# A two-layer hybrid encoder: tiles moved by 64 bytes, S5 tables made by doubling, norm rows stored from ScalarE's queue, first raw weights in freed slots

## The chip, the cores and the metric

The kernel runs on one core of one Trainium2 chip. Its engines are TensorE (PE in the profile; PEld is its weight load), VectorE (DVE), ScalarE (ACT), GpSimd (POOL) and SyncE (SP), which issues most DMAs. The metric is the device time of one execution in microseconds, as the median of several runs.

## The reference, cut to what matters

Two layers, 512 rows of 1024. Four mixers read x, a gate weights each, a projection and a layer norm follow, then a SwiGLU FFN of width 2816 and a second layer norm.

```python
h = x @ w_in[l]
branches = (o_ret, o_att, o_gla, o_s5)
mixed = sum(sigmoid(x @ w_gate[l, b] + b_gate[l, b]) * (branches[b] @ w_branch[l, b]) for b in range(4))
x = layer_norm(ALPHA * x + mixed @ w_out[l], ln1_g[l], ln1_b[l])
ffn = (silu(x @ w_ffn_gate[l]) * (x @ w_ffn_up[l])) @ w_ffn_down[l]
x = layer_norm(ALPHA * x + ffn, ln2_g[l], ln2_b[l])
# in o_s5, a diagonal complex state: ab = mag * exp(i * theta), x[t] = ab * x[t-1] + bu[t]
```

For S5 the kernel uses tables of cos and sin of t * theta for t = 0 to 511, in 8 groups of 128 states (`er`, `ei`).

## The kernel before, in words

Every float32 product is made of three products of a high part and a rest in the format fp32r (`wh` and `wl` for a weight, `XH` and `XL` for x): `split` (L202) writes the high part on ScalarE (a CAST) and the rest on VectorE. Weights come by `wload` (L343): a DMA into `wr` (two buffers) on SyncE's queue, then the split into `wh` and `wl`, which a priority puts ahead of other work; the Tile scheduler orders the rest by dependence and by the order of the code. Each engine, and SyncE's queue, works in that fixed order.

A layer goes through these stages. *Mixers and gates* (`phase("mx", MIXERS)`, L1178): projections, four mixers and a stream of gate products `pg` and branch products `pb`, which add up in 8 tiles `acc`. *Projection* `proj_ln` (L508) with `wo`: 8 slices k, four blocks t of 128 rows, products `pj`; the last 4 slices are done block by block, with `layer_norm` (L417) after each block. Its `rest` (L449) stores the normalised rows to `xsp` in DRAM, transposes them on TensorE (`tp`), scales them (`xf`) and splits them into `XH` and `XL`; `block_sums` (L479) makes from the blocks the operands `bh`, `bl` of a Strassen-like scheme. *FFN* `ffn` (L1069): 22 slices f; `weights` (L1077) loads `raw` (128x2048) and `ws` (128x1024, to which a second, adding DMA on GpSimd's queue comes), makes `s24` on GpSimd and splits into `wh`/`wl` (twice), `wkh`/`wkl` and `fh`/`fl`; `product` (L1104) is 12 matmuls of 256 columns, of which each slice has seven (`fa`, `fb`, `fc`). The heads of the first two slices (`PRE = 2`) stand ahead of the rest; that of the first needs only `raw` and the first two blocks of x. *Down-projection*: `proj_ln` with `wdn`, 22 slices k, the operands `aph`, `apl` split from the FFN's `g`. In layer 0 it also makes layer 1's S5 tables, by `tables(k)` (L1167): `s5_constants(1)` at k = 0, then at each even k from 2 to 16 `s5_table` on GpSimd, out of a table of 32 and one of 16 angles (`eb`, `ea`) that `s5_constants` (L244) leaves to GpSimd. The two results are stored to `esp` in DRAM from SyncE's queue (L1173).

Tiles lie in pools; a phase's pool begins behind the pools that are always there. Before the change, `XH`, `XL`, the pairs `b` and all tiles of the phases (`fh`, `fl`, `wkh`, `wkl`, `aph`, `apl`, the `a` slots) begin at a multiple of 128 bytes in each partition, `wr`, `wh` and `wl` 64 bytes past one.

## Time and profile before

| | |
|---|---|
| median of 3 runs | 1786.33 us (1785.63 to 1788.24) |
| the profiled execution | 1790.67 us, its span 1788.8 us |
| PE, PEld, DVE, ACT, POOL busy | 92%, 84%, 68%, 40%, 31% of the span |
| mean granted TensorE clock | 0.962 of full speed |

The profile is of one execution; its span goes from the first to the last instruction. Engines overlap, so their shares don't add up. A row of the timeline gives the start, the duration, the instruction (output<-inputs, x count for several in a row), and in brackets the idle time before it and what ended it. Most rows name L126, the helper that records operations, so rows are told apart by tiles. All times of all views are in us from the span's start.

### The profile page before, as it was taken

How to read it: one execution, taken by the hardware profiler on the slowest of the kernel's cores; microseconds unless marked ns; L12 is line 12 of the kernel's file. 1: busy time of each engine (PE TensorE's matmuls, PEld its weight loads, DVE VectorE, ACT ScalarE, POOL GpSimd, SP SyncE). 2: the span in 40 equal slices, each digit the busy share in tenths (PEclk: the TensorE clock that was granted, in tenths of full speed). 3: DMA queues.
4: the chain of work that ended last, by engine and by line, in shares of the span. 5: the costliest groups of instructions: out<-in, count | busy, mean ns of one | idle time of the engine just before them, and what ended most of it. 6: DMA issues, size and time to landing. Idle time of an engine off the chain costs nothing. (4 is left out here: it accounts for less than half of the span.)

```text
span 1788.8 us, 27714 instructions
## 1 busy us (share of the span) xinstructions
PE 1641.2 (92%) x11068; PEld 1503.4 (84%) x11068; DVE 1224.6 (68%) x1801; ACT 711.1 (40%) x1200; POOL 550.4 (31%) x503
## 2 busy tenths in 40 slices
PE   8999998989969999984799999999999689999997
PEld 7988887878859999963589989888898589999786
DVE  4766468988587777671364656689876777786635
ACT  4453342233354444420243554533333444444321
POOL 0601015650043444189400000022204534442602
PEclk9999999989989999996899999999999899999999
DMA  6522212222357767322435423134333577773522
GB/s 204 186 93 82 79 60 73 85 90 95 112 172 203 226 202 223 100 101 94 141 120 193 155 70 121 58 95 136 114 106 132 168 207 206 217 209 116 177 95 82
DMA packets 82785, 241.46 MB, mean 135 GB/s; under 512 B 8352, under 2 KB 8544, under 8 KB 77024
## 3 DMA queue, kind: packets, MB, share of 16 engines
q1 hardware_dynamic: 70688, 216.63, 35.7%
q0 software_dynamic: 11968, 23.07, 7.5%
q8 instruction: 86, 1.41, 0.3%
q14 instruction: 43, 0.35, 0.1%
HBM read 220.79 MB, written 18.87 MB: 134 GB/s over the span
## 5 line engine op out<-in xcount | busy, mean ns | idle before, releaser
L126 DVE TENSOR_TENSOR wl<-wr,wh 128x1024 fp32r<-128x1024 f32 (+2 forms) x162 | 205.0, 1267 | 296.9 <-ACT wh L126 284.8
L126 ACT CAST wh<-wr 128x1024 fp32r<-128x1024 f32 (+2 forms) x162 | 164.9, 1020 | 360.8 <-PE pg L126 103.8
L126 PE MATMUL pg<-XH,wh 128*128 128x256 f32 x1024 | 150.1, 288 | 1.3 <-DVE sg L126 1.2
L126 PE MATMUL pg<-XL,wh 128*128 128x256 f32 x1024 | 146.9, 284 | 0.0
L126 PEld LDWEIGHTS pg<-XH,wh 128*128 128x128 f32 x1024 | 139.7, 196 | 8.5 <-DVE sg L126 2.6
L126 PE MATMUL pg<-XH,wl 128*128 128x256 f32 x1024 | 144.9, 282 | 0.0
L126 PE MATMUL pj<-wh,aph 128*128 128x512 f32 x320 | 106.8, 409 | 39.4 <-ACT wh L126 37.1
L126 POOL TENSOR_TENSOR s<-ws,raw 128x512 f32<-128x512 f32 x44 | 66.4, 1508 | 231.7 <-DMA ws<-in_wgu 117.2
L126 PEld LDWEIGHTS pg<-XL,wh 128*128 128x128 f32 x1024 | 134.2, 194 | 1.0
L126 PEld LDWEIGHTS pg<-XH,wl 128*128 128x128 f32 x1024 | 132.0, 191 | 0.7
L126 POOL TENSOR_TENSOR acc<-acc,sg 128x512 f32<-128x512 f32 x32 | 60.3, 1887 | 170.7 <-DVE sg L126 170.7
L126 PE MATMUL pj<-wh,apl 128*128 128x512 f32 x320 | 105.6, 404 | 4.4 <-DVE apl L126 4.4
L126 PEld LDWEIGHTS pj<-wh,aph 128*128 128x128 f32 x320 | 62.3, 197 | 55.1 <-ACT wh L126 39.2
L126 PE MATMUL pj<-wl,aph 128*128 128x512 f32 x320 | 105.1, 402 | 0.3 <-DVE wl L126 0.3
L126 POOL TENSOR_TENSOR s<-s,raw 128x512 f32<-128x512 f32 x44 | 78.6, 1787 | 3.5
L126 PEld LDWEIGHTS pj<-wh,apl 128*128 128x128 f32 x320 | 62.0, 195 | 19.8 <-DVE apl L126 6.2
L1084 POOL DMA_DIRECT2D ws<-in_wgu x44 | 52.9, 1213 | 81.5 <-DMA ws<-in_wgu 81.5
L126 POOL TENSOR_TENSOR x<-x,lg 128x512 f32<-128x512 f32 x27 | 41.3, 1542 | 117.5 <-DMA lg<-in_lng 112.0
L126 ACT CAST wkh<-raw 128x512 fp32r<-128x512 f32 x44 | 27.3, 620 | 126.1 <-PE fa L126 124.6
L126 PEld LDWEIGHTS pj<-wl,aph 128*128 128x128 f32 x320 | 61.7, 194 | 15.8 <-DVE wl L126 1.9
L126 POOL TENSOR_TENSOR hr<-hv,ct 128x8 f32<-128x8 f32 x8 | 13.4, 1670 | 183.5 <-DVE hv L126 183.5
L126 DVE TENSOR_TENSOR wkl<-raw,wkh 128x512 fp32r<-128x512 f32 x44 | 41.3, 939 | 38.2 <-ACT wkh L126 38.1
(382 smaller groups left out, 4371.3 us busy)
## 6 DMA issues: line engine op xcount, KB each, us to landing
wr<-in_wt SPq DMA_DIRECT2D x90, 512.0 KB
raw<-in_wgu SPq DMA_DIRECT2D x44, 1024.0 KB
ws<-in_wgu SPq DMA_DIRECT2D x44, 512.0 KB
ws<-in_wgu POOLq DMA_DIRECT2D x44, 512.0 KB, 6.4
wr<-in_wdn SPq DMA_DIRECT2D x44, 512.0 KB
bwr<-in_wbr SPq DMA_DIRECT2D x32, 256.0 KB
wr<-in_wo SPq DMA_DIRECT2D x16, 512.0 KB
skr<-spr SPq DMA_DIRECT2D x32, 192.0 KB
```

The lines of the kernel that those rows point to most:

```text
L126: r = fn(out, *a, **kw)
L1084: nc.gpsimd.dma_start(s13.rearrange("p (a c) -> p a c", a=2), bc(wgu[l, f][:, 1024:1536].unsqueeze(1), [P, 2, 512]), accum_op=ALU.add)
```

## The change

It makes `PAD` and two small pads around the pools: `XH`, `XL` (`xp`) and the pairs (`bp`) come first, at a multiple of 128 bytes; `wp` and, by the last pad of 64 bytes, all phases' tiles 64 bytes past one. Layer 1's 16-angle table is no longer made; `s5_doubled` copies 32 angles from `eb` on ScalarE and doubles them four times on VectorE (two TENSOR_SCALAR and two SCALAR_TENSOR_TENSOR a level, with the turns `pr`, `pi`), and stores to `esp` from GpSimd's queue. `xsp` is stored from ScalarE's queue, behind the scaling in the code. The gates' tiles get a phase of their own (`mg`), closed with `mx`; the FFN's two `raw` tiles get one (`fr`), which lies over the gates'. Some mixer tiles move to kept tiles or pairs, and `tc.issue_after` places four loads of the mixers and the residual behind the latest noted weight load.

```diff
--- before.py
+++ after.py
@@ -37,12 +37,15 @@
-MIXERS = {"a": 37, "sg": 7, "acc": 8}
+MIXERS = {"a": 37}
+GATES = {"sg": 7, "acc": 8}
 HELD = {"g": 22}
-FFN = {"raw": 2, "s24": 2, "fh": 2, "fl": 2, "wk": 4, "po": 6}
+FFN = {"s24": 2, "fh": 2, "fl": 2, "wk": 4, "po": 6}
+RAW = {"raw": 2}
 DOWN = {"x": 10, "ap": 6, "ws": 8, "a": 6}
 WIDE = {"raw": 2048, "s24": 1024, "fh": 1024, "fl": 1024}
 PAIRS = 6
+PAD = 16
@@ -145,11 +148,20 @@
     def pool(name, bufs, **kw):
         return ctx.enter_context(tc.tile_pool(name=name, bufs=bufs, **kw))
+    def pad(i, n):
+        pool(f"pad{i}", 1).tile([P, n], F32, name=f"pad{i}")
+    xp = pool("xp", 1)
+    bp = pool("bp", PAIRS)
+    pad(0, 16)
     cp = pool("cp", 1)
+    pad(1, 16)
     wp = pool("wp", 3)
     sm = pool("sm", 2)
-    bp = pool("bp", PAIRS)
     lp = pool("lp", 1)
+    pad(2, PAD)
     psm = pool("psm", 3, space=bass.MemoryType.PSUM)
     psx = pool("psx", 5, space=bass.MemoryType.PSUM)
     dr = pool("dr", 1, space=bass.MemoryType.DRAM)
@@ -220,8 +232,8 @@
         return ((ah, bh), (ah, bl), (al, bh))
-    XH = cp.tile([P, 8, S], F32R, name="XH")
-    XL = cp.tile([P, 8, S], F32R, name="XL")
+    XH = xp.tile([P, 8, S], F32R, name="XH")
+    XL = xp.tile([P, 8, S], F32R, name="XL")
     def load_x(k):
         r = slot("xr")
@@ -303,7 +315,7 @@
         eb, ea = slot("eb"), slot("ea")
         vb = lambda a, i, n: a[:, NJ * n * i:NJ * n * (i + 1)].rearrange("p (j n) -> p j n", n=n)
         tabs = [vb(ea, 0, 16), vb(ea, 1, 16), vb(eb, 0, 32), vb(eb, 1, 32)]
-        for (er, ei, k0, lv) in ((*tabs[2:4], 0, 5), (*tabs[0:2], 5, 4)):
+        for (er, ei, k0, lv) in ((*tabs[2:4], 0, 5), (*tabs[0:2], 5, 4))[:2 - l]:
             G.memset(er[:, :, 0:1], 1.0)
             G.memset(ei[:, :, 0:1], 0.0)
             for k in range(lv):
@@ -318,7 +330,7 @@
                 G.tensor_tensor(uu, ei[:, :, 0:n], c, ALU.mult)
                 G.tensor_tensor(ei[:, :, n:2 * n], er[:, :, 0:n], s, ALU.mult)
                 G.tensor_tensor(ei[:, :, n:2 * n], ei[:, :, n:2 * n], uu, ALU.add)
-        return mag, cfr, cfi, tabs
+        return mag, cfr, cfi, tabs, (pr, pi)
     esp = dr.tile([8, 2, P, 512], F32, name="esp")
@@ -336,6 +348,23 @@
         G.tensor_tensor(v3(tn), ai, br_, ALU.mult)
         G.tensor_tensor(ei, ei, tn, ALU.add)
         return er, ei
+    def s5_doubled(j, tabs, turns):
+        pr, pi = turns
+        er, ei, t = slot("er"), slot("ei"), slot("et")
+        A.copy(er[:, 0:32], tabs[2][:, j, :])
+        A.copy(ei[:, 0:32], tabs[3][:, j, :])
+        for k in range(5, 9):
+            n = 2 ** k
+            c, s = (x[:, 8 * k + j:8 * k + j + 1] for x in (pr, pi))
+            t1, t2 = t[:, 0:n], t[:, 256:256 + n]
+            V.tensor_scalar(t1, ei[:, 0:n], s, None, ALU.mult)
+            V.tensor_scalar(t2, ei[:, 0:n], c, None, ALU.mult)
+            V.scalar_tensor_tensor(er[:, n:2 * n], er[:, 0:n], c, t1, ALU.mult, ALU.subtract)
+            V.scalar_tensor_tensor(ei[:, n:2 * n], er[:, 0:n], s, t2, ALU.mult, ALU.add)
+        for i, x in enumerate((er, ei)):
+            nc.gpsimd.dma_start(esp[j, i], x)
     wdma = [None]
@@ -447,8 +476,6 @@
                 V.tensor_scalar(xh[h], xh[h], mv[:, 0:1], rs, ALU.subtract, ALU.mult)
         def rest():
-            for h in range(2):
-                SP.dma_start(xsp[P * t:P * t + P, 512 * h:512 * h + 512], xh[h])
             tp = [mx_ps("tp") for _ in range(2)]
             xf = [kept(f"xf{h}") if sums is not None and t == 1 else
                   slot("xf", tag="g" if sums is not None and t == 3 else "a") for h in range(2)]
@@ -466,6 +493,8 @@
                     else:
                         A.activation(xf[h][:, cols], tp[h][:, cols], AF.Identity, bias=b, scale=g)
             for h in range(2):
+                nc.scalar.dma_start(xsp[P * t:P * t + P, 512 * h:512 * h + 512], xh[h])
+            for h in range(2):
                 if sums is None or t < 2 or h == 1:
                     split(XH[:, 4 * h:4 * h + 4, P * t:P * t + P],
@@ -499,7 +528,8 @@
         gb = None if scaled else ln_params(l, which, tag)
         for t in range(4):
             for h in range(2):
-                SP.dma_start(xh[t][h], src[P * t:P * t + P, 512 * h:512 * h + 512])
+                with tc.issue_after(wdma[0].ins):
+                    SP.dma_start(xh[t][h], src[P * t:P * t + P, 512 * h:512 * h + 512])
                 if gb:
                     G.tensor_tensor(xh[t][h], xh[t][h], gb[0][h], ALU.mult)
                     G.tensor_tensor(xh[t][h], xh[t][h], gb[1][h], ALU.add)
@@ -578,10 +608,11 @@
         far = pt[:, l, S_FAR:S_FAR + 4]
         nbs, nbt, brs_, pr = [], [], [], {}
         for p in range(2):
-            nb = slot("nb")
+            nb = kept(f"x{p}")
             nbt.append(nb)
             nbs.append(nb.rearrange("p (e c) -> p e c", e=2))
-            SP.dma_start(nbs[p], nbias[l, :, 2 * p:2 * p + 2, :])
+            with tc.issue_after(wdma[0].ins):
+                SP.dma_start(nbs[p], nbias[l, :, 2 * p:2 * p + 2, :])
             x = pair("br")
             brs_.append((x[:, 0:512], x[:, 512:1024]))
@@ -674,8 +705,9 @@
         return y
     def retention(q, k, v, gate2, br):
-        dt = slot("dt")
-        SP.dma_start(dt, dtab)
+        dt = kept("xf0")
+        with tc.issue_after(wdma[0].ins):
+            SP.dma_start(dt, dtab)
         qs, ks, raw = {}, {}, {}
         def load(h):
@@ -733,7 +765,7 @@
                 T.transpose(ps[:, P * t:P * t + P], o[:, P * t:P * t + P], ident)
             f = slot("hf")
             V.scalar_tensor_tensor(f, ps, 0.5, gate2[p], ALU.mult, ALU.mult)
-            br[p] = split_slots("br", f)
+            br[p] = split_pair("br", f)
     def gla_in(pss):
@@ -829,7 +861,7 @@
                 T.transpose(ps[:, P * t:P * t + P], o[t // 2][:, c:c + P], ident)
             f = slot("hf")
             V.scalar_tensor_tensor(f, ps, 0.5, gate2[p], ALU.mult, ALU.mult)
-            br[p] = split_slots("br", f)
+            br[p] = split_pair("br", f)
     def s5(l, s5c, uspr, br):
@@ -845,7 +877,7 @@
             V.tensor_tensor(b[64:96, :], r[64:96, :], b[64:96, :].bitcast(F32), ALU.subtract)
             bst[c] = b
-        mag, cfr, cfi, small = s5c
+        mag, cfr, cfi, small, _ = s5c
         c_f, cc, t_ = slot("scf"), slot("scc"), slot("sct")
         SP.dma_start(c_f, sc[l])
         yield [c_f]
@@ -1080,7 +1112,7 @@
             r = slot("raw", tag="raw")
             s13 = wp.tile([P, 1024], F32, tag="wr", name=nm("ws"), bufs=2)
             SP.dma_start(s13, wgu[l, f][:, 0:1024])
-            SP.dma_start(r, wgu[l, f])
+            wdma[0] = SP.dma_start(r, wgu[l, f])
             nc.gpsimd.dma_start(s13.rearrange("p (a c) -> p a c", a=2),
                                 bc(wgu[l, f][:, 1024:1536].unsqueeze(1), [P, 2, 512]),
                                 accum_op=ALU.add)
@@ -1169,13 +1201,13 @@
         if k == 0:
             s5c_[0] = s5_constants(1)
         elif k % 2 == 0 and k <= 16:
-            for i, x in enumerate(s5_table(k // 2 - 1, s5c_[0][3])):
-                SP.dma_start(esp[k // 2 - 1, i], x)
+            s5_doubled(k // 2 - 1, *s5c_[0][3:5])
     rest = None
     for l in range(L):
         phase("mx", MIXERS)
+        phase("mg", GATES)
         tt_ = lambda i, s: gemm_t(wt[l, i], s)
         pv = gemm_n(w2[l, 0], 512, load_x if l == 0 else None, rest)
@@ -1237,11 +1269,14 @@
             parts.append([pair(x).rearrange("p (k c) -> p k c", c=256) for x in ("bh", "bl")])
         rest = proj_ln(l, 0, mix, 8, wo[l], 4, 2, xh, None, None, False, ([], parts))
         close()
+        close()
         phase("hd", HELD)
         phase("ff", FFN)
+        phase("fr", RAW)
         gs = ffn(l, parts, rest)
+        close()
         close()
         phase("dn", DOWN)
         xh = residual(l, 0, xsp, False)
```

In the order that results, three places follow.

SyncE, layer 0's down-projection (`wr` from `in_wdn` are the slices' weights), first before the change:

```order
L126 DMA wr1431_8550<-in_wdn 128x1024
L126 DMA wr1436_8584<-in_wdn 128x1024
L126 DMA esp_83<-er1413_8434 128x512
L126 DMA wr1445_8630<-in_wdn 128x1024
L126 DMA esp_83<-ei1414_8435 128x512
L126 DMA esp_83<-er1427_8514 128x512
L126 DMA esp_83<-ei1428_8515 128x512
L126 DMA wr1450_8664<-in_wdn 128x1024
```

and now:

```order
L129 DMA wr1427_8565<-in_wdn 128x1024
L129 DMA wr1432_8599<-in_wdn 128x1024
L129 DMA wr1440_8656<-in_wdn 128x1024
L129 DMA wr1445_8690<-in_wdn 128x1024
L129 DMA wr1453_8747<-in_wdn 128x1024
```

The stores have left this queue.

ScalarE and VectorE at slice k5 of the same stage now (`wh1428`, `wl1429`, `aph1430` and `apl1431` are k5's, `er1411`, `ei1412` the first table, `eb1399` GpSimd's table). ScalarE:

```order
L129 CAST aph1422_8514<-g1056_6097 128x512
L129 COPY er1411_8427<-eb1399_8325 128x32
L129 CAST aph1469_8844<-g1182_6965 128x512
L129 COPY ei1412_8428<-eb1399_8325 128x32
L129 COPY er1424_8518<-eb1399_8325 128x32
L129 CAST wh1428_8566<-wr1427_8565 128x1024
```

VectorE, from the first table's third level:

```order
L129 TENSOR_SCALAR et1413_8429<-ei1412_8428,s5w1395_8280 128x128 x2
L129 SCALAR_TENSOR_TENSOR er1411_8427<-er1411_8427,s5w1395_8280,et1413_8429 128x128
L129 SCALAR_TENSOR_TENSOR ei1412_8428<-er1411_8427,s5w1395_8280,et1413_8429 128x128
L129 TENSOR_TENSOR wl1429_8567<-wr1427_8565,wh1428_8566 128x1024
L129 TENSOR_SCALAR et1413_8429<-ei1412_8428,s5w1395_8280 128x256 x2
L129 SCALAR_TENSOR_TENSOR er1411_8427<-er1411_8427,s5w1395_8280,et1413_8429 128x256
L129 SCALAR_TENSOR_TENSOR ei1412_8428<-er1411_8427,s5w1395_8280,et1413_8429 128x256
L129 TENSOR_TENSOR apl1431_8572<-g1074_6221,aph1430_8571 128x512
```

Before the change nothing of the tables stood on these two engines between the slices.

SyncE, layer 0's projection with `wo` and the FFN's first loads, before:

```order
L126 DMA wr914_5148<-in_wo 128x1024
L126 DMA wr921_5158<-in_wo 128x1024
L126 DMA wr926_5168<-in_wo 128x1024
L126 DMA ws962_5422<-in_wgu 128x1024
L126 DMA ws983_5501<-in_wgu 128x1024
L126 DMA xsp_84<-x877_4992 128x512
...
L126 DMA xsp_84<-x1884_4999 128x512
L126 DMA raw961_5421<-in_wgu 128x2048
L126 DMA raw982_5500<-in_wgu 128x2048
```

and now:

```order
L129 DMA wr911_5162<-in_wo 128x1024
L129 DMA raw959_5439<-in_wgu 128x2048
L129 DMA raw980_5518<-in_wgu 128x2048
L129 DMA wr918_5172<-in_wo 128x1024
L129 DMA wr923_5182<-in_wo 128x1024
L129 DMA ws960_5440<-in_wgu 128x1024
L129 DMA ws981_5519<-in_wgu 128x1024
```

The two `raw` loads went ahead of the last two weight loads, and the eight `xsp` stores are gone from here.

## Rows read from the trace of the kernel before

**Rows 1.** By stage: us; PE, PEld, DVE, ACT, POOL busy; PEclk; DMA share; GB/s.
```profile
759.00:935.50 176.50, 135.52 (x546) 106.95 (x547) 80.21 (x114) 42.58 (x67) 100.22 (x121) 0.87 0.33 113
1657.30:1779.70 122.40, 121.58 (x528) 98.96 (x528) 64.61 (x73) 36.08 (x48) 35.12 (x24) 1.00 0.35 121
```
**Rows 2.** Waits of PE, 755 to 940 us (engine, line, releaser: us, times, longest).
```profile
PE pj L126 <- ACT wh L126: 37.1, 5, 16.1
```
**Rows 3.** Timeline of PE, layer 0's down-projection (start us, us, instruction, idle before).
```profile
789.63 0.63 PE L126 MATMUL pj<-wh,aph 128*128 128x512 f32 x2
...
818.28 1.22 PE L126 MATMUL pj<-wh,aph 128*128 128x512 f32 x2 [16.10 <-ACT wh L126]
...
878.39 0.62 PE L126 MATMUL pj<-wh,aph 128*128 128x512 f32 x2
```
**Rows 4.** Timeline of SyncE, the same stage.
```profile
813.46 0.33 SPq L126 DMA_DIRECT2D esp<-er  x1
813.88 0.37 SPq L126 DMA_DIRECT2D wr<-in_wdn  x1
```
**Rows 5.** Timeline of GpSimd, the same stage.
```profile
802.67 0.46 POOL L126 TENSOR_TENSOR eb<-eb,ea 128x128 f32<-128x128 f32 x1
```
**Rows 6.** Timeline of VectorE, the same stage.
```profile
760.88 0.68 DVE L126 TENSOR_TENSOR apl<-g,aph 128x512 fp32r<-128x512 f32 x1
761.48 0.19 DVE L126 TENSOR_SCALAR s5w<-s5w 128x72 f32<-128x72 f32 x1
...
774.90 1.24 DVE L126 TENSOR_SCALAR nr<-nr 128x8 f32<-128x8 f32 x1
...
782.67 3.46 DVE L126 TENSOR_TENSOR apl<-g,aph 128x512 fp32r<-128x512 f32 x2
```
**Rows 7.** Groups of VectorE by form, whole span (x count, busy us, mean ns, idle before).
```profile
L126 DVE SCALAR_TENSOR_TENSOR gs<-gs,gc 128x256 f32<-128x256 f32 x8 | 3.8, 478 | 0.0
...
L126 DVE TENSOR_SCALAR pp<-pp,as 128x256 f32<-128x256 f32 x8 | 3.0, 375 | 0.2
```
**Rows 8.** Timeline of SyncE, the start of layer 0's FFN.
```profile
519.16 5.05 SPq L126 DMA_DIRECT2D raw<-in_wgu  x2
```
**Rows 9.** Timeline of PE, the starts of the FFN in layers 0 and 1.
```profile
525.38 1.22 PE L126 MATMUL fa<-XH,wh 128*128 128x256 f32 x4 [11.31 <-ACT wh L126]
...
539.99 0.64 PE L126 MATMUL fb<-bh,wh 128*128 128x256 f32 x4
...
1423.82 1.22 PE L126 MATMUL fa<-XH,wh 128*128 128x256 f32 x4 [14.95 <-ACT wh L126]
...
1438.59 0.62 PE L126 MATMUL fb<-bh,wh 128*128 128x256 f32 x4
```
**Rows 10.** Timeline of VectorE, the start of layer 0's FFN.
```profile
523.77 3.44 DVE L126 TENSOR_TENSOR fl<-ws,fh 128x1024 fp32r<-128x1024 f32 x2
527.13 2.28 DVE L126 TENSOR_TENSOR wl<-raw,wh 128x1024 fp32r<-128x1024 f32 x1
...
533.25 1.21 DVE L126 TENSOR_TENSOR wl<-raw,wh 128x1024 fp32r<-128x1024 f32 x1
534.39 1.35 DVE L126 TENSOR_SCALAR xf<-tp,pt 128x128 f32<-128x128 f32 x4
```
**Rows 11.** Timeline of PE, layer 0's attention projections, first and last of 17 groups.
```profile
43.92 1.07 PE L126 MATMUL aq<-XL,wh 128*128 128x256 f32 x8
...
59.33 0.84 PE L126 MATMUL ak<-XH,wh 128*128 128x256 f32 x6
```
**Rows 12.** Timeline of PE, one slice of layer 0's FFN: 9 groups, then 12.
```profile
640.76 0.64 PE L126 MATMUL fc<-XH,fh 128*128 128x256 f32 x4
...
645.08 0.63 PE L126 MATMUL fc<-XH,wh 128*128 128x256 f32 x4
...
650.73 0.52 PE L126 MATMUL fc<-XH,fh 128*128 128x256 f32 x3
```
**Rows 13.** Waits of PE, 60 to 466 us (layer 0's mixers), the first of the list.
```profile
PE sv L126 <- ACT stk L126: 6.9, 3, 4.7
```

## The prediction

> **What bounds the kernel now.** I read the busy shares first (in the table above): TensorE 92% of the span, VectorE, the next, 68%. So a gain must either close one of TensorE's gaps or make its matmuls themselves shorter. The second view is a table by stage. Both layers run the same down-projection (22 slices of k, called k0 to k21 below, then a layer norm), yet it takes 176.5 us in layer 0 and 122.4 us in layer 1; the reader is to compare the PE busy column (135.52 against 121.58) and the granted clock (0.87 against 1.00) of the two rows [rows 1].
>
> The third view is the list of waits of layer 0's down-projection: 37.1 us in five waits of `pj` for the cast `wh` on ACT, the longest 16.1 [rows 2]. The timeline says why. ACT's cast is late because its weight load is late: SyncE issues the load at 813.88, just behind the store `esp<-er` at 813.46, which had to wait for GpSimd's table [rows 4]. TensorE starts k5 at 789.63, stands 16.10 us before k7 and has its last such wait behind it at 878.39, where k12 starts [rows 3]. The starts of the FFN come third; their rows are read with part 2.
>
> **Part 1, the S5 tables.** Removed: 48 table operations of 512 columns and the 24 small ones of the 16-column table on GpSimd, and the 16 stores from SyncE's queue. So no weight load stands behind a table any more. If nothing else came in, the stage would take layer 1's 122.4 us, a gain of 54. But something does, and it is in the order excerpts: ACT's copy `er1411<-eb` stands ahead of the cast `wh1428` of k5, and VectorE's first table ahead of `wl1429` and `apl1431` of k5. So k5 now waits for GpSimd's 32-column table, which it never did. That table's last operation ends at 803.13 [rows 5]; ahead of it on GpSimd stand 16 operations on the residual, which the change leaves, so I don't move it.
>
> From 803.1 on: ACT has three copies of 32 columns and a cast of 512, 1.1 us by my estimate (VectorE takes 0.68 for 512 columns [rows 6]), then the cast of 1024, about as much again, so `wh` is there by 805.3. On VectorE, levels 32, 64 and 128 are twelve operations. A TENSOR_SCALAR of 72 columns takes 0.19 beside an idle GpSimd [rows 6], one of 256 columns 0.375, a SCALAR_TENSOR_TENSOR of 256 columns 0.478 [rows 7]; from these I estimate 0.17, 0.19, 0.26 and 0.37 for the first kind at 32, 64, 128 and 256 columns, 0.20, 0.23, 0.28 and 0.48 for the second, less 0.07 each, by which neighbours overlap (an `apl` of 0.68 and its follower start 0.60 apart [rows 6]). Twelve come to 1.8 us, the last four to 1.4, a table to 3.3. So: VectorE begins near 804.0, `wl1429` (1.21, as the `wl` in [rows 10]) ends at 807.0, level 256 at 808.4, `apl1431` (0.68) at 809.1. TensorE can run only the first pair of k5 before that pair's `apl`, so k5 is in effect at 809.1 - 0.46 = 808.6 instead of 789.63.
>
> From there a k is 24 matmuls: layer 1 had 528 of them in 121.58 us [rows 1], 5.5 a k. Restarting at half clock adds about 2 us, by the two matmuls of 1.22 with which k7 starts, where two otherwise end in 0.62 [rows 3], for three such pairs. So k12 starts near 808.6 + 7 x 5.5 + 2 = 849 instead of 878.39, 29 us earlier, and what follows is the same. While the tables are made, VectorE has 10 `wl`, 13 `apl` and 8 tables, 12.1 + 8.8 + 26.4 = 47 us for ten k of 55 us; this hides, but its order holds some `apl` behind a whole table, for which I take back 2. **Term: -27.** Bounds: -33, if the table ends 4 us earlier for want of neighbours; -17, if VectorE paces the stage (a rival). GpSimd's 16 stores lie where it idles, and what queues behind them, the layer norm's `rs`, comes after the last table. ACT's 16 copies lie beside TensorE.
>
> **Part 2, the starts of the FFN.** In layer 0 the stores `xsp<-x` of SyncE run ahead of `raw` and hold it until 519.16 [rows 8]. TensorE idles 11.31 us before the first `fa` at 525.38, and 14.95 in layer 1 before 1423.82 [rows 9]. Now `raw` lies over `acc`, free when the gates end, and is issued between weight loads of the projection; its cast and its `wl` stand before the layer norms. So `fa` can follow `pj` at about 514. That does not earn 11 us, since the next product is bound by another chain: the last token block's `xf` on VectorE begins at 534.39, behind the two `wl` of the first slices, the second ending at 534.46 [rows 10]. In the new order only `wkl`, one `fl` and one `wl` from `s24` stand between the layer norm and `xf`; without the second `fl` (1.7), the first `wl<-raw` (2.2) and the second (1.2) it starts 5 to 6 us earlier, and with it the first `fb`, 539.99 before [rows 9]. I take 5.5 there and 1.5 of the later short gaps. Layer 1's first `fb` came at 1438.59, 14.95 + 14.77 = 29.7 us after TensorE had stopped, against 25.9 in layer 0; levelled, it gains 3.8 more, 9.3 in all, of which I take 9. **Term: -16.** Bounds: -8 (only `xf`'s 5.5 and a part of layer 1's) and -26 (the two long waits whole). Of ACT's 24 stores at 0.33 us, the issue time on SyncE [rows 4], none makes a new wait: ACT's next work in that place needs the same normalised rows through the transposes.
>
> **Part 3, where the weights lie.** The rows show three paces for 256 columns. In layer 0's attention projections 17 groups of eight start from 43.92 to 59.33: 113.3 ns a matmul [rows 11]. In the FFN the nine groups of four with `fh`, `fl` and `wk` take 640.76 to 645.08, 120.0 ns; the twelve with `wh` and `wl` take 645.08 to 650.73, 117.7 ns [rows 12]. In the kernel's placement `wh` and `wl` lie 64 bytes past a multiple of 128, and `XH`, `XL` and the `b` pairs on one; `fh`, `fl` and `wk` lie on one, too. So the slow groups are those with both operands alike. After the change all three move to 64. Per FFN there are 36 such matmuls in each of 22 slices, 1,584 in both layers, and 2,112 others. If they join the 117.7 of their neighbours: 1,584 x 2.3 = 3.6 us. If all 3,696 fall to 113.3, which the projections have with the same placement and no 120-group ahead of them: 1,584 x 6.7 + 2,112 x 4.4 = 19.9. No row decides; I take half the matmuls at each pace. **Term: -11.8.** The projections' stationary slices move to 64 under moving weights at 64: alike, so perhaps slower. Per 256 columns the differences above are 2.3 and 4.4 ns; 1,248 matmuls of 512 columns at -2.3 to +2.3 ns are 2.9 to either side; I take 0.
>
> The trace has this difference, 2.3 to 6.7 ns on a matmul. The Trainium skill (TensorE: Matmul & The Clock Gate, section "Step-by-step: what each phase is for") says that streaming operand and weight load have two independent read ports, so that loading the next weights takes no bandwidth from the running matmul. By that the placement would earn nothing and the sum would be 43, not 55; rows 12 speak against it, but they show groups that differ in their tiles as well.
>
> **Part 4, the rest.** Gates get a phase of their own, `nb`, `dt` and two branches other slots, and four loads another place in SyncE's queue. In layer 0's mixers the costliest wait of TensorE is 6.9 us in three times, for `stk` on ACT [rows 13], and no transfer is in the list that it heads, so an earlier or later table load has nothing to win; the cover is the S5 chain through ACT and VectorE. A new order there can win or lose about that costliest wait in each of the two layers: 14 to either side, taken as 0.
>
> **The sum.** -27 - 16 - 11.8 = -54.8. The profiled execution took 1790.67, 4.3 above the median of 1786.33, so it becomes 1735.9 there and **1731.5** as a median.
>
> **Rivals.**
> (a) The placement does not matter to TensorE: the third term is gone, 1743. For it: the slow groups sit on other tiles too. Against: nine groups in a row at exactly 120.0, and the step back at 645.08.
> (b) All FFN matmuls fall to 113.3: 8.1 more, 1723.
> (c) VectorE paces the tables. If a table takes 4.4 us (no overlap) and `wl` and `apl` 1.3 and 1.0, as they do beside GpSimd, the ten k need 13 + 13 + 35 = 61 us, 6 more than TensorE's 55; I take 10, since the order lets some of it fall on a k without slack: 1742.
> (d) The FFN starts gain only 8: 1740.
> (e) Slower: VectorE is held up by GpSimd. At 774.90, beside GpSimd's residual work, a VectorE operation of 8 columns took 1.24 us, and two `apl` 3.46 instead of 1.28 [rows 6]. If the 128 new operations went that way beside GpSimd's 16 descriptor-writing stores, they would cost 128 x 1.2 = 154 us, with the 26 of (c) 180 instead of 55: 125 lost, 1857. It decides at about 0.66 us an operation (110 us less 26, over 128), where the loss eats the whole 55. Against: GpSimd has only the stores left, and VectorE's operations beside an idle GpSimd took 0.19. The Trainium skill (SBUF, section "SBUF: two separate sides") calls the port that VectorE and GpSimd share an exclusive lock, held for a whole instruction; the 1.24 agrees with that.
>
> **How the numbers follow.** Forecast (within 6 us) 0.45; (a) 0.18; (b) 0.12; (c) 0.10; (d) 0.09; (e) 0.02; both signs of the mixers 0.04. Below: tables -33, starts -22, FFN -20 give 1711. Above: (c) with (a) gives 1753. The range is 1710 to 1755. One measurement tells some 0.2%, 3.6 us, from no change; only (e) or several mishaps together with the mixers reach that: faster 0.94, same 0.03, slower 0.03.
>
> **What would show it.** Part 1: no `esp` row on SyncE; one wait of some 15 to 20 us before k5, ended by the table's chain, and none of 3 us or more after it; a stage of about 147 us. Part 2: first `fa` right behind `pj`, `fb` some 22 us behind it. Part 3: no 120.0 in the FFN; a slice in 9.5 to 9.9 us where it takes 9.97 now. The prediction is wrong if k5 waits under 8 or over 30 us, if the mixers' waits change by over 14 us, or if the FFN's pace stays.

## The result, and the profile after

The changed kernel takes **1744.09 us** (median of 4 runs, 1743.43 to 1746.49) against 1786.45 for the kernel before beside it: a ratio of 0.9764, 95% interval 0.9747 to 0.9781, or 42.4 us. 1731.5 was forecast, with a range of 1710 to 1755. The profiled execution's span is 1741.7 us against 1788.8.

By the page of the profile after, TensorE is busy for 94% of the span (92% before), VectorE for 71% (68%), ScalarE for 41% (40%) and GpSimd for 28% (31%).

For the following table each span was cut where TensorE starts the first matmul of a stage (timeline of PE); layer 0's mixers count from the span's start, layer 1's down-projection to the start of its last `pj`; all in us. The last columns are kernels of the experiments.

| stage | before | after | `pads_only` | `tables_only` | `shift_again` | `shift_best` |
|---|---|---|---|---|---|---|
| mixers, layer 0 | 467.1 | 465.8 | 467.8 | 465.8 | 463.8 | 465.0 |
| last `pj` of `wo` to first `fb`, layer 0 | 27.2 | 24.9 | 27.1 | 27.2 | 24.3 | 24.4 |
| FFN, layer 0 | 219.0 | 216.5 | 216.6 | 217.0 | 211.4 | 220.2 |
| down-projection, layer 0 | 177.1 | 143.6 | 175.9 | 143.3 | 141.7 | 125.2 |
| mixers, layer 1 | 425.8 | 426.5 | 428.9 | 425.8 | 423.7 | 424.2 |
| last `pj` of `wo` to first `fb`, layer 1 | 31.0 | 24.1 | 31.2 | 30.7 | 24.3 | 24.3 |
| FFN, layer 1 | 218.7 | 216.9 | 215.8 | 218.7 | 218.6 | 214.1 |
| down-projection, layer 1 | 122.0 | 120.7 | 120.7 | 122.0 | 120.7 | 120.7 |

So of the profiled 47.1 us, 33.5 lie in layer 0's down-projection, 9.2 at the starts of the FFN (2.3 + 6.9), 4.3 in the two FFNs and 1.3 in layer 1's down-projection; mixers, `wo` and the tail together give back 1.2. The medians differ by 42.4: the profiled execution of the kernel before was 4.3 above its median and that of the changed kernel 0.7 below, and the rows don't tell in which stage. A row can differ by some 2 us between executions: `tables_only` changes nothing in layer 0's mixers and FFN, and they take 1.3 and 2.0 us less there than in the first column.

**The tables.** The two down-projections after, by stage (columns as in [rows 1]):

```profile
753.00:896.60 143.60, 126.72 (x552) 103.42 (x553) 103.14 (x243) 45.42 (x84) 42.10 (x65) 0.94 0.41 138
1610.80:1731.40 120.60, 119.77 (x527) 98.89 (x528) 63.81 (x72) 35.49 (x48) 34.96 (x23) 1.00 0.36 122
```

VectorE's column has grown from 80.21 to 103.14, GpSimd's has fallen from 100.22 to 42.10, and the granted clock has risen from 0.87 to 0.94. The waits of PE in that stage, all of them:

```profile
PE pj L129 <- ACT aph L129: 12.4, 2, 11.2
PE pj L129 <- DVE apl L129: 5.6, 3, 2.9
```

37.1 us for `wh` [rows 2] are gone; in their place stands one wait before k5 and a rest of it. The timeline of PE shows both:

```profile
795.09 1.22 PE L129 MATMUL pj<-wh,aph 128*128 128x512 f32 x2 [11.24 <-ACT aph L129]
799.18 1.22 PE L129 MATMUL pj<-wh,apl 128*128 128x512 f32 x2 [2.87 <-DVE apl L129]
```

What they wait for, in the timeline of GpSimd (the last operation of the 32-angle table, then the first store) and of VectorE (the first of the four levels of the first table):

```profile
792.75 0.45 POOL L129 TENSOR_TENSOR eb<-eb,ea 128x128 f32<-128x128 f32 x1
798.74 0.63 POOL L367 DMA_DIRECT2D esp<-er  x1 [5.54 <-DVE ei L129]
```

```profile
793.48 0.39 DVE L129 TENSOR_SCALAR et<-ei,s5w 128x32 f32<-128x32 f32 x2 [13.29 <-ACT ei L129]
793.78 0.25 DVE L129 SCALAR_TENSOR_TENSOR er<-er,s5w,et 128x32 f32<-128x32 f32 x1
```

The table ends at 793.20, 40.2 us after the stage's start at 753.03; before it was 803.13 - 759.0 = 44.1 [rows 1, 5]. VectorE, which stands still for 13.29 us in front of it, had been busy beside it. The timelines of GpSimd have the same pair of table operations, before the change and now:

```profile
794.73 1.93 POOL L126 TENSOR_TENSOR eb<-eb,s5w 128x32 f32<-128x32 f32 x2
```

```profile
786.86 0.44 POOL L129 TENSOR_TENSOR eb<-eb,s5w 128x32 f32<-128x32 f32 x2
```

With the last pair of additions to the residual (3.95 us before, beside two `apl`; 2.50 now) this is 2.9 of the 3.9 us.

**The starts of the FFN.** SyncE, PE (both layers), then ACT, GpSimd and VectorE in layer 0, each from its timeline:

```profile
473.71 0.91 SPq L129 DMA_DIRECT2D raw<-in_wgu  x2
```

```profile
512.60 0.72 PE L129 MATMUL fa<-XH,wh 128*128 128x256 f32 x4
...
529.57 1.22 PE L129 MATMUL fa<-XH,wkh 128*128 128x256 f32 x4 [10.72 <-ACT fu L129]
...
536.52 0.62 PE L129 MATMUL fb<-bh,wh 128*128 128x256 f32 x4
...
1393.90 1.05 PE L129 MATMUL fb<-bh,wh 128*128 128x256 f32 x4
```

```profile
528.20 1.04 ACT L129 CAST wh<-s 128x1024 fp32r<-128x1024 f32 x1 [5.41 <-POOL s L129]
529.15 0.37 ACT L129 COPY fu<-fa 128x256 f32<-128x256 f32 x1
```

```profile
523.16 3.79 POOL L129 TENSOR_TENSOR s<-ws,raw 128x512 f32<-128x512 f32 x2 [2.49 <-DVE bl L129]
526.91 2.48 POOL L129 TENSOR_TENSOR s<-s,raw 128x512 f32<-128x512 f32 x2
```

```profile
529.28 1.22 DVE L129 TENSOR_TENSOR wl<-s,wh 128x1024 fp32r<-128x1024 f32 x1 [3.45 <-ACT wh L129]
530.42 1.36 DVE L129 TENSOR_SCALAR xf<-tp,pt 128x128 f32<-128x128 f32 x4
```

`raw` is issued 45 us earlier than in [rows 8], and the first `fa` follows the transposes without a wait (512.60, where [rows 9] had 11.31 idle). But the 10.72 us come back one product later: ACT copies `fu` only at 529.15, behind the cast `wh<-s`, which waits for GpSimd's sums, which wait for the last `bl`. `xf` starts at 530.42, right behind the `wl` of these sums [rows 10].

**The pace.** Attention projections of layer 0, two starts that are 18 groups of eight apart, and one slice of layer 0's FFN (timeline of PE):

```profile
43.71 1.10 PE L129 MATMUL aq<-XH,wh 128*128 128x256 f32 x8
...
60.67 1.10 PE L129 MATMUL ak<-XH,wh 128*128 128x256 f32 x8
...
640.03 0.63 PE L129 MATMUL fc<-XH,wh 128*128 128x256 f32 x4
...
645.68 0.63 PE L129 MATMUL fc<-XH,fh 128*128 128x256 f32 x4
...
649.92 0.63 PE L129 MATMUL fc<-XH,wh 128*128 128x256 f32 x4
```

From start to start: (60.67 - 43.71) / 144 = 117.8 ns in the projections, 113.3 before [rows 11]; 117.7 for the 48 with `wh`, `wl` and 117.8 for the 36 with `fh`, `fl`, `wk`, 117.7 and 120.0 before [rows 12]. All of these now have one pace. For the two FFNs the pace alone makes (120.0 - 117.8) x 1,584 = 3.5 us.

### The profile page after: what moved, and what is told of

It reads as the page before. It is cut to its first block, busy times and chain, and to the rows that moved or that the text cites. A ratio compares the mean times of both kernels' runs of the same rounds, so it can differ in the third digit from the quotient of the medians.

```text
span 1741.7 us, 27826 instructions
## 1 busy us (share of the span) xinstructions
PE 1628.8 (94%) x11068; PEld 1501.1 (86%) x11068; DVE 1244.8 (71%) x1929; ACT 713.1 (41%) x1216; POOL 492.9 (28%) x445
## 5 line engine op out<-in xcount | busy, mean ns | idle before, releaser
L129 PE MATMUL pj<-wh,aph 128*128 128x512 f32 x320 | 102.7, 395 | 13.6 <-ACT aph L129 13.6
L129 DVE TENSOR_TENSOR fl<-ws,fh 128x1024 fp32r<-128x1024 f32 x44 | 61.0, 1387 | 10.5 <-ACT fh L129 10.4
```

The costliest lines, as they stand in the source:

```text
L129: r = fn(out, *a, **kw)
```

## The experiments

### The placement

`pads_only` is the kernel before with the new pools and pads alone (`PAD = 16`).

> The kernel before with the change's pools and pads and nothing else. Theory (placement): no 120.0 ns left in the FFN, its 1,584 slow matmuls at 117.7, so -3.6 us; the 512-column matmuls of the projections at 226.7 as after the change, 2.3 less on 1,440, so -3.3; the projections of the mixers' 113.3 perhaps at 117.7, on about 1,250 matmuls, so 0 to +5.6. Together -7 to -1: 1779 to 1785 us. Rival (a), placement does nothing: the FFN's groups stay at 120.0 and the time at 1786 within 1.5 us.

Measured: 1787.74 us, ratio 0.9996 (0.9982 to 1.0010). The FFNs win 2.4 and 2.9 us and the down-projections 1.2 and 1.3; the mixers give 0.7 and 3.1 back. The timeline of PE shows where, in the attention projections again:

```profile
43.23 1.10 PE L127 MATMUL aq<-XH,wh 128*128 128x256 f32 x8
...
60.20 1.10 PE L127 MATMUL ak<-XH,wh 128*128 128x256 f32 x8
```

117.8 ns. The paces are those of the theory; its 1779 to 1785 us are missed by 3, and the time is near the rival's, whose reason is not the case. The placement's part of the change is worth nothing that stands clear of the noise (between 3.2 us less and 1.8 more), since what the FFN and the down-projection win the mixers' products lose.

`pace_table` measures the pace by itself: long rows of matmuls, each with its weight load, without transfers between them, at start offsets chosen per group.

```diff
+                T.matmul(ps[:, o:o + n], W[:, s + P * k:s + P * k + P], X[:, m0:m0 + n],
+                         start=(c == 0), stop=(c == 8 * reps - 1), skip_group_check=True)
```

> A kernel of its own: none of the reference's work, only rows of 48 (256 columns) or 32 (512 columns) matmuls with a weight load each, from one tile W and one tile X that both begin at a multiple of 128 bytes, read at offsets of 0, 32, 64, 96, 128 or 192 bytes; what it writes to the output is no result. Theory, that the place decides: with 256 columns, weights and moving rows both on a multiple of 128, or both 64 past one, take about 120.0 ns a matmul, and 64 apart 117.7 or 113.3; the same pair of offsets gives the same pace in all three turns. Rival, that the place does not matter: all offsets give one pace within 1 ns, or a pace that differs between turns for one and the same pair. Second theory, that the pace is kept from what ran before: rows that follow another pair without a gap keep the pace of that pair.

Measured, in the timeline of PE, 48 matmuls of 256 columns a group (the stationary operand's start lies 0, 64, 192 bytes from the moving one's, modulo 256), and three groups of 24 and 48 in a row (`pk` and `pa`: offset 0 then 64; `pl`: offset 0 then 192):

```profile
22.87 6.01 PE L186 MATMUL na<-X,W 128*128 128x256 f32 x48 [0.68 <-ACT e L189]
29.39 5.72 PE L186 MATMUL nb<-X,W 128*128 128x256 f32 x48 [0.52 <-ACT e L189]
...
42.12 5.92 PE L186 MATMUL nd<-X,W 128*128 128x256 f32 x48 [0.52 <-ACT e L189]
...
589.21 8.60 PE L186 MATMUL pk<-X,W 128*128 128x256 f32 x72 [0.73 <-ACT e L189]
598.54 8.58 PE L186 MATMUL pl<-X,W 128*128 128x256 f32 x72 [0.73 <-ACT e L189]
607.85 8.78 PE L186 MATMUL pa<-X,W 128*128 128x256 f32 x72 [0.73 <-ACT e L189]
```

From start to start, past the first eight of a group, this is 120.0 ns at offset 0, 113.3 at 64, 118.7 at 128 and 117.8 at 192, the same in three turns and in whichever of the two operands the shift lies. For 512 columns it is 227.2, 233.3, 232.2 and 229.0. There is also a history. The second theory, that a row keeps the pace of the row before it, fits only `pe` of the rows whose offset changes (64, then 192, 113.4 ns in both; not shown). Behind matmuls at offset 0, offset 64 runs at 117.8 (`pa`) and offset 192 at 113.3 (`pl`), the other way round than alone. In both the stationary operand's place changes, as it does in the kernels. Where the moving operand's place changes instead, it is the other way round again: 113.4 at 64 (`pk`), 117.7 at 192 (`pb`, not shown). So 64 and 192 have the same two paces, and here what ran before decides between them; offset 0 came to 120.0 behind every row. Why is open. With this table the kernels can be read. Before: `wh` against `XH` at 64 gives the projections' 113.3; in the FFN `fh` and `wk` lie at 0 (120.0) and `wh` comes behind them at 64 (117.7). After: all at 192, 117.8. For `pj` the stationary operand is `aph`: offset 192 before, 0 after, means of 229.6 and 226.9 ns.

`no_pad` puts the phases' tiles back on multiples of 128, the order of all instructions being that of the change:

```diff
-PAD = 16
+PAD = 32
```

> The changed kernel with a last pad of 128 bytes in place of 64, so that all phases' tiles lie at a multiple of 128 again, and nothing else changes, not even the order. Theory: the FFN's groups with fh, fl and wk go back to 120.0 (+3.6 us) and the projections to about 229 (+3.3): 1749 to 1752 us. Rival: within 1.5 us of 1744.

Measured: 1747.93 us, ratio 0.9767 (0.9748 to 0.9787). One slice of layer 0's FFN (timeline of PE):

```profile
639.89 0.64 PE L129 MATMUL fc<-XL,fh 128*128 128x256 f32 x4
...
643.73 0.62 PE L129 MATMUL fc<-XH,wh 128*128 128x256 f32 x4
...
649.17 0.64 PE L129 MATMUL fc<-XH,fh 128*128 128x256 f32 x4
```

120.0 ns with `fh` (offset 0), but 113.3 with `wh` (offset 192 behind offset 0), as `pl` has it. The FFN's gain is lost at `pj`, which lies at offset 64 here: 232.9 ns against 226.9, so that the ratio is that of the change (0.9764). The expectation (1749 to 1752) had `fh` right, but neither `wh` nor the size at `pj`.

`shift_128` moves weights and phases together by 128 bytes, so that all products of 256 columns lie at offset 64 and `pj` stays at 0; `shift_again` is the same kernel once more, on another chip.

```diff
-    pad(1, 16)
+    pad(1, 48)
```

> The changed kernel with its weights and all phases' tiles moved on by another 128 bytes, the same instructions in the same order. Theory, from the pace table: what counts is how far the weights begin behind the moving rows, modulo 256 bytes: 64 gives 113.3 ns for 256 columns, 192 gives 117.8, and the changed kernel has 192. Now 64: the FFN's 3,696 matmuls lose 4.4 ns each (16.3 us), the mixers' 1,250 projections 4.5 (5.6), the 3,072 gate products 3.9 (12), less 1 to 2 for the branch products: 1709 to 1716 us. Rival 1: only the place modulo 128 counts, and the time stays at 1744 within 2. Rival 2: the FFN is held by VectorE or by its transfers at the old pace, and only the projections and gates gain: 1724 to 1730.

> The kernel of shift_128 once more, so that the next two stand beside it on one chip. Theory (at offset 64 the pace of an FFN is kept from how it was entered): 1722 to 1734 us, and in the profiled execution each FFN lies at 113 to 114 or at 117.8 ns a product throughout, not between; which of the two layers it is may change. Rival (layer 0's FFN is slow by its tiles): layer 0 at 117.8, layer 1 at 113.5 again.

Measured: 1730.61 us, 0.9682 (0.9657 to 0.9707), and 1730.62 us, 0.9674 (0.9645 to 0.9702): 13 to 14 us faster than the change, less than half of what the table promised. Of that promise 16.3 us lay in the FFNs and some 16 in the mixers; by the table of stages, `shift_again` won 3.4 and 4.8. Why the mixers gave so little was not followed up. After its start, layer 0's FFN ran at 117.8 in `shift_128` and layer 1's at 113.3; in `shift_again` it was the other way round, so it is not the tiles. Nor is the pace settled by how an FFN is entered, as I had expected; the timeline of PE in layer 0's FFN of `shift_again` has a point where it turns:

```profile
704.38 0.62 PE L129 MATMUL fa<-XL,wh 128*128 128x256 f32 x4
...
708.91 0.62 PE L129 MATMUL fa<-XH,wkl 128*128 128x256 f32 x4
709.47 0.74 PE L129 MATMUL fb<-bh,fh 128*128 128x256 f32 x4
710.05 0.63 PE L129 MATMUL fb<-bl,fh 128*128 128x256 f32 x4
...
714.76 0.64 PE L129 MATMUL fa<-XH,wl 128*128 128x256 f32 x4
```

Ten groups of four take 4.53 us (113.3 ns) up to 708.91, ten take 4.71 (117.8) from 710.05, and between them lie two gaps of a tenth of a microsecond, one product apart, in the row of products. I followed this FFN and both FFNs of `shift_best` (the same placement) product by product: the pace changes at such gaps, in either direction, and nowhere else; behind other gaps it stays. What in a gap decides is open.

### The tables

`tables_only` is the kernel before with `s5_doubled` and the stores from GpSimd's queue alone.

> The kernel before with the doubled tables and their stores on GpSimd's queue, and nothing else. Theory: layer 0's down-projection takes 143 to 146 us instead of 177, with one wait of some 11 us at k5 and one of some 3 behind it, and the time is 1786.4 - 33 = 1753 us (1750 to 1757). Rival: a part of the 33 came from the other parts, and the gain is under 27 (over 1759).

Measured: 1754.38 us, ratio 0.9802 (0.9776 to 0.9829). The stage takes 143.3 us, as in the change: both lie where they were expected, and this part is worth all that the stage gained, without help from the others.

`table_first` puts GpSimd's residual operations behind its 32-angle table.

```diff
+            with tc.issue_after(last_g[0].ins):
+                for f in late:
+                    f()
```

> The changed kernel with GpSimd's 16 operations on the residual behind the 32-angle table instead of ahead of it. Theory: k5's wait for the table was 11.2 us, and 2.9 for apl behind it, and some 1.6 of half clock: they go, and 1744 becomes 1728 to 1732. Rival: GpSimd now works on the residual while VectorE doubles, which holds VectorE's operations, and the gain is under 8 (over 1736).

Measured: 1744.88 us, 0.9764 (0.9736 to 0.9791), no gain. The table ends 20 us earlier in the stage (at 768.31, where the stage starts at 748.0), but then GpSimd's residual work runs beside VectorE's doubling. Timeline of VectorE, the same operation beside that work and after it:

```profile
770.77 1.34 DVE L129 SCALAR_TENSOR_TENSOR er<-er,s5w,et 128x32 f32<-128x32 f32 x1
...
793.31 0.25 DVE L129 SCALAR_TENSOR_TENSOR er<-er,s5w,et 128x32 f32<-128x32 f32 x1
```

The first table takes from 768.60 to 791.15 in this way, and TensorE waits for the `apl` behind it (timeline of PE):

```profile
791.81 1.22 PE L129 MATMUL pj<-wh,apl 128*128 128x512 f32 x2 [7.16 <-DVE apl L129]
```

So the rival was the case. 1.34 us is rival (e)'s price, twice its deciding 0.66; the change itself was spared it because there the 32-angle table, and so the doubling, stands behind GpSimd's residual work.

`shift_early` goes on from `shift_128`: the 32-angle table is made piece by piece during layer 0's FFN, and the doubled tables come at other k.

```diff
+LATE = (6, 8, 9, 10, 12, 13, 14, 16)
...
+            if l == 0 and f >= 4:
+                next(early, None)
```

> shift_128 with layer 1's 32-angle table made piece by piece during layer 0's FFN (in tiles that are free there), and the eight doubled tables at k = 6, 8, 9, 10, 12, 13, 14, 16 of the down-projection. Theory: what is left of the tables' cost is the wait for the 32-angle table, so the stage from the down-projection's first product to layer 1's first projection falls from 143 us to 124 to 128 (layer 1's takes 120.7), no wait for wh or apl over 3 us is left, layer 0's FFN stays within 1 us, and the time falls by 15 to 19 us against shift_again. Rival: VectorE beside GpSimd's residual operations, and bunched tables, take half of it back: a stage of 131 to 135 us with waits for apl of 3 us and more.

Measured: 1738.36 us, 0.9711 (0.9688 to 0.9734), 8 us slower than `shift_again`. The stage falls only to 137.1 us, and layer 0's FFN rises to 226.9 (in one wait of TensorE for `wh` of 6.5 us, where the whole table came in one piece after all). Both the theory and the rival's size were off. Timelines of VectorE, of GpSimd (first and last of 6 rows, ten operations) and of PE in the stage:

```profile
774.84 0.24 DVE L130 SCALAR_TENSOR_TENSOR er<-er,xf,et 128x32 f32<-128x32 f32 x1
775.01 12.94 DVE L130 SCALAR_TENSOR_TENSOR ei<-er,xf,et 128x32 f32<-128x32 f32 x1
```

```profile
775.48 1.30 POOL L130 TENSOR_TENSOR x<-x,lb 128x512 f32<-128x512 f32 x1
...
786.64 1.25 POOL L130 TENSOR_TENSOR x<-x,lg 128x512 f32<-128x512 f32 x1
```

```profile
790.77 1.22 PE L130 MATMUL pj<-wh,aph 128*128 128x512 f32 x2 [6.39 <-ACT aph L130]
```

An operation that takes 0.24 us took 12.94: it ended at 787.95, GpSimd's ten operations at 787.89, as if it had not been let in once between them. The Trainium skill (SBUF — State Buffer, section "SBUF: two separate sides") has the port that VectorE and GpSimd share as an exclusive lock for the length of one instruction. The 1.34 us of `table_first` agree with that, one operation of 1.25 us being waited for; one such hold does not explain the 12.94, since ten instructions passed in that time. What let them pass is not shown.

`shift_best` takes both stalls out by order alone: pieces of the small table tied to slices, doubled tables first, the residual operations behind the last `esp` store.

```diff
+LATE = (1, 2, 4, 5, 7, 8, 10, 11)
...
+                with tc.issue_after(vi.ins), tc.issue_after(last_g[0].ins):
+                    next(early, None)
...
+                with tc.issue_after(last_s[0].ins):
+                    for f in late:
+                        f()
```

> shift_early with its two stalls taken out by order alone: the pieces of the 32-angle table are tied one to a slice of layer 0's FFN (behind that slice's sum on GpSimd and its g on VectorE), the doubled tables come at k = 1, 2, 4, 5, 7, 8, 10, 11, and GpSimd's 16 residual operations stand behind the last esp store, so that no table operation of VectorE meets a run of them. Theory (what cost shift_early its gain was one small VectorE operation that got the port only after GpSimd's whole run, 12.94 us, and the table in one piece in the FFN): no VectorE operation of the tables over 2 us, no wait of TensorE over 3 us in the stage, the stage 122 to 126 us against 141.7 in shift_again and 137.1 in shift_early, layer 0's FFN 210 to 213 or, at the slow pace, 217 to 219 us, and the time 1707 to 1722 us. Rival (VectorE's work, doubling and splits together, paces the first twelve k's): waits for apl of 3 us and more in several k's, a stage of 130 us and more.

Measured: **1722.17 us**, ratio 0.9636 (0.9617 to 0.9655), faster than both kernels: 64.5 us less than before, where the change saves 42.4, and 0.2 above the range that was expected. Its stage by windows, and all waits of PE from 740 to 880:

```profile
755.05:880.20 125.15, 124.28 (x552) 102.67 (x553) 95.60 (x205) 44.63 (x82) 40.33 (x35) 0.99 0.47 158
```

```profile
PE pj L130 <- ACT aph L130: 1.2, 1, 1.2
PE pj L130 <- DVE apl L130: 0.9, 1, 0.9
```

The stage takes 125.2 us, 4.5 more than layer 1's, at a granted clock of 0.99. Of the 16.5 us that it wins on `shift_again`, layer 0's FFN gives 8.8 back: TensorE still has two waits of 2.69 and 1.08 us (up to 674.77 and 677.41), behind a load that GpSimd issues only after the largest piece of the small table (at 664.92); some 20 products behind them run at the lower clock level, and some 330 products from 588 to 628 ran at 117.8 ns.

### The starts of the FFN

`s24_freed` lays `s24` over the gates' tiles, beside `raw`:

```diff
-FFN = {"s24": 2, "fh": 2, "fl": 2, "wk": 4, "po": 6}
-RAW = {"raw": 2}
+FFN = {"fh": 2, "fl": 2, "wk": 4, "po": 6}
+RAW = {"raw": 2, "s24": 2}
```

> The changed kernel with s24 over the gates' freed slots, too, like raw, so that GpSimd need not wait for the block sums' slots. Theory: in the changed kernel the first fb is held by s24, ready at 528 in layer 0, and by wl and xf behind it on VectorE; with s24 ready before the layer norms' end xf starts some 4.6 us earlier, and so does fb, in both layers: 1731 to 1736. Rival: fb is held by the block sums on VectorE anyway, and the gain is under 4 (over 1740).

Measured: 1754.96 us, 0.9834 (0.9807 to 0.9861), 11 us slower than the change. The first `fb` does come 3.3 us nearer to the last `pj` in layer 0 (21.6 us) and 0.7 in layer 1, but the projections with `wo` take 52.2 and 54.5 us where the change has 45.8 and 46.7. GpSimd and VectorE, in the middle of `wo`:

```profile
499.74 1.25 POOL L129 TENSOR_TENSOR s<-ws,raw 128x512 f32<-128x512 f32 x1 [6.84 <-DMA ws<-in_wgu]
...
501.73 1.03 POOL L129 TENSOR_TENSOR rs<-ve,ct 128x1 f32<-128x1 f32 x1
```

```profile
502.80 1.94 DVE L129 TENSOR_SCALAR x<-x,mv,rs 128x512 f32<-128x512 f32 x2 [6.71 <-POOL rs L129]
```

The sum, now free to go early, stands ahead of the layer norm's `rs` in GpSimd's order and waits 6.84 us for a transfer; `rs` waits behind it. Neither the theory nor the rival had this.

`stores_sync` puts the `xsp` stores back on SyncE's queue, with `raw` still over the gates' tiles (two lines in `rest`).

> The changed kernel with the norm rows' stores back on SyncE's queue, raw still in the freed slots. Theory: what let raw go ahead was its slot, not the queue; with raw ahead of the stores in SyncE's order, the time stays: 1742 to 1747. Rival: the stores hold the loads of the FFN's third slice behind them, and the start of each FFN costs 3 us or more: over 1749.

Measured: 1745.07 us, 0.9770 (0.9745 to 0.9795): the same. The slot let `raw` go ahead, not the stores' move.

`shift_early_s24` takes the tiles `fh`, `fl` ahead of `s24`, so that `fh` lies over the block sums in its place.

```diff
+            fh, fl = (slot(t, F32R, t) for t in ("fh", "fl"))
             s24 = slot("s24", tag="s24")
```

> shift_early with the tiles fh and fl taken ahead of s24, so that s24 lies over weight tiles that are free early and fh over the block sums. Theory (GpSimd's sum for s24 waits for the last block sums, and through the cast wh<-s holds ACT's copy of fa): from the last pj of wo to the first fb 22 to 23 us instead of 24.9 in layer 0 and 24.0 in layer 1, the projection with wo unchanged at 45 to 47, 3 to 5 us less in all than shift_early. Rival (the order of ACT and of GpSimd, not the slot, holds it): no change over 1 us.

Measured: 1740.93 us, 0.9726 (0.9703 to 0.9749); 23.7 and 23.6 us to the first `fb` against 24.3 and 23.2 in `shift_early`: nothing, as the rival said, for a reason that neither named. ACT and VectorE in layer 0:

```profile
523.05 1.04 ACT L130 CAST fh<-ws 128x1024 fp32r<-128x1024 f32 x1 [4.42 <-DVE bl L130]
```

```profile
517.93 5.09 DVE L130 TENSOR_TENSOR bl<-bs,bh 128x512 fp32r<-128x512 f32 x3
```

GpSimd's sums do start earlier, but beside them the three `bl` take 5.09 us where they took 1.88 in the change (from 521.14) and in `shift_early`; what the one engine wins the other loses.

## Why the prediction was right, and where it was off

The time lies in the range and, by the table of stages, every part has the sign forecast for it, but the gain is 12 us smaller than the 54.8 of the sum. That it isn't further off is in part luck: part 1 won 6.5 us more than its term and part 2 won 6.8 less. What is left is part 3, and the 4.7 us between the profiled pair and the medians.

**Part 1** said -27, with -33 "if the table ends 4 us earlier for want of neighbours". It measured -33.5, and the table ends 3.9 us earlier: the bound was the case. The step that failed is that I took the table's end over from 803.13 although my own part had VectorE stand idle in front of it. GpSimd's own operations became shorter for it. 14.1 us of waits around k5 (a little under the forecast 15 to 20, as the table is earlier), 3.6 us a table (3.3 forecast), no later wait of 3 us, a stage of 143.6 (147): the mechanism was as described, and `tables_only` shows that it is this part's alone. The 2 us that I took back for `apl` behind tables did not come. Rivals (c) and (e) did not happen; (e)'s price is real (`table_first`, `shift_early`), and only the order of the work kept it away.

**Part 2** said -16 and measured -9.2, near its bound of -8. `raw`, the first `fa` at 512.60 and the three operations taken off VectorE's order were as forecast. What failed is the step "only `wkl`, one `fl` and one `wl` from `s24` stand between the layer norm and `xf`": I counted VectorE's operations and not what the last of them waits for. It waits 3.45 us for a cast that waits 5.41 for GpSimd, so `xf` won 2.8 us against the last `pj`, not 5 to 6. So the first `fb` came 24.9 and 24.1 us behind `pj`, not some 22. Rival (d), a gain of 8, is near in size; that a bound of GpSimd follows at once was in none of my rivals. Two ways of moving one tile of this chain, `s24_freed` and `shift_early_s24`, did not make the kernel faster. No run makes part 2 alone; its size is read from the stages, and the 42.4 less the 34 of `tables_only` leave about as much.

**Part 3** said -11.8 and measured -4.3 in the FFNs, of which the pace makes 3.5, the smaller of the two cases that the term lies between; the -1.3 in layer 1's down-projection and the mixers' losses make it nothing in all (`pads_only`). Two steps failed. "I take half the matmuls at each pace": none fell to 113.3. And of the projections I counted only the 1,248 matmuls of 512 columns (2.9 us to either side), not the mixers' products of 256 columns, which went from 113.3 to 117.8. The reading behind both, that the slow groups are "those with both operands alike", holds as far as it goes: offset 0 came to 120.0 in all rows of `pace_table`. What it missed is that unlike operands have two paces and that 64 bytes either way are not the same: the change has 192, which alone runs at 117.8, where the projections before had 64 and 113.3. Rival (a)'s 1743 is nearest to the result, but not by its reason: the placement matters to TensorE, the change only picked a place where gains and losses cancel. `shift_128` is the one where they don't.

The Trainium skill (TensorE: Matmul & The Clock Gate, section "Step-by-step: what each phase is for") has independent read ports for the streaming operand and the weight load. That the placement would earn nothing, as the prediction reads it, is not what `pace_table` measured: one kind of instruction, no other engine at work within a group, and 113.3 to 120.0 ns by the offset of the two.

**Part 4** was taken as 0 within 14 to either side; the mixers moved by -1.3 and +0.7, which is within what two executions differ by.

## What to carry to other kernels

Before costing a moved operation, follow what its inputs wait for on every engine, not only what stands ahead of it on its own; here the new bound was one step back. Keep small VectorE operations out of a stretch where GpSimd has a row of operations queued: another order of the same operations won 12 us in one stage (137.1 to 125.2). Where TensorE is 90% busy, measure its pace over the operands' offsets before choosing a placement, for all products at once, since what one shape wins another may lose.

## What the runs showed that I had not expected

- The pace of a matmul depends on the offset of its two operands modulo 256 bytes: 113.3 to 120.0 ns for 256 columns, 227 to 233 for 512, and of the offsets tried the best for one is the worst for the other (64).
- At offsets 64 and 192 there are two paces, 113.3 and 117.8, and in `pace_table` what ran before decides between them; in the FFNs at 64 a stretch of products keeps one until some gap, which can be as short as a tenth of a microsecond. The profiled executions of `shift_128` and `shift_again` differ in it; that it is what spreads the times of one kernel (1722.28 to 1734.05 us in the runs of `shift_128`) is not shown.
- A VectorE operation of 32 columns can stand through a whole row of GpSimd operations (12.94 us), or alternate with them one by one (1.34 us).
